# Thirteen Strassen pairs instead of eight in the up product of an FFN, and the gate product moved behind a spill

## The chip, the core and the metric

The kernel runs on one core of a Trainium2 chip. Its engines work side by side, each with a queue that it takes in order: TensorE (PE: matmul, with its weight loads as PEld), VectorE (DVE), ScalarE (ACT), GpSimd (POOL), and SyncE (SP), which issues the DMAs. A scheduler fixes the order in each queue when the program is built. The metric is the device time of one launch in microseconds; the kernel before takes 855.47 us, the median of three runs from 853.64 to 856.37.

## The reference, cut to what matters

One layer over 512 tokens of width 1024: a mixer (an mLSTM branch and an S5 branch), a residual with layer norm, and then a feed-forward block with a causal convolution of three taps on its gate:

```python
FFN_HIDDEN = ((8 * D_MODEL // 3 + 127) // 128) * 128      # 2816 = 22 tiles of 128
def _conv_glu_ffn(h, w_ffn_up, w_ffn_conv, b_ffn_conv, w_ffn_down):
    val, gate = jnp.split(h @ w_ffn_up, 2, axis=-1)
    gate = jax.nn.gelu(_causal_dwconv(gate, w_ffn_conv, b_ffn_conv))
    return (gate * val) @ w_ffn_down
...
    x = _layer_norm(ALPHA * x + (1.0 + g1) * mix, ln1_gain[l], ln1_bias[l])
    h = _standardize(x) * (1.0 + sc2) + sh2
    f = _conv_glu_ffn(h, w_ffn_up[l], w_ffn_conv[l], b_ffn_conv[l], w_ffn_down[l])
    x = _layer_norm(ALPHA * x + (1.0 + g2) * f, ln2_gain[l], ln2_bias[l])
```

sh1 to g2 are six rows of 1024 that come from a second input c by a matrix (w_ada); g2 is one of them and multiplies the block's result.

## The kernel before

**Arithmetic.** Every large product is taken in three passes: each fp32 operand is split into a rounded high part (an ACT cast, L226 for weights) and a low part (a DVE subtraction, L215), and mm3 (L247 to L249) adds high·high, high·low and low·high. Weights come by DMA into a tile w, which wsplit turns into wh and wl.

**Stages.** The mixer takes the first 440 us. Then tail_product runs the mix product, a running sum over k whose last steps are kept back so that the four token tiles t = 0 to 3 end one after the other; finish1 adds the residual x (two loads of 256 KB into hx for each tile) and norms it (post), and h2tr transposes the result, the first half of the tokens and then the second half. The up product follows. Its 22 hidden tiles are called pairs here: pair j has a gate tile and a value tile of 128 rows each. Pairs 0 and 1 are computed in token halves while the norm of the last tile still runs; 2 and 3 are ordinary pairs, which is 48 matmuls of 512 columns. From j = 4 on, fast_and_plain takes a Strassen pair and an ordinary one together, eight times, with their matmuls interleaved. A Strassen pair is seven products (prod, L1287) of 12 matmuls of 256 columns, 84 in all; its weights are combined by four DVE operations (fast_operands) and each of the seven operands is split by half (an ACT cast, L1250, and a DVE subtraction). The gate goes through gate_half (bias, convolution with two DVE operations, gelu2 with two more and two on ACT) and is multiplied by the value in val_half, on DVE. The results of pairs 0 to 17 are spilled to DRAM; 18 to 21 stay on the chip as split operands.

**Down product.** tail_product again, over the 22 pairs in the order 18, 19, 0 to 17, 20, 21: 14 steps of 24 matmuls, and eight that are kept back. act_at loads a spilled pair and splits it; scaled multiplies each row of down weights by g2 with two DVE operations before the split. finish2 and post add the residual and norm.

**g2.** Its row is summed on DVE from 16 loads (ada2_step, part q = 3: a tensor_scalar L201 at kc = 0, then scalar_tensor_tensor L207), spread over the up product by MODS, and grow_in_place (four matmuls, L963, with casts and splits on both sides) spreads the sum over the partitions at j = 16.

**What sets the order.** Tile pools: a load waits until the tile that last had its slot has been read (hh has 7 slots, s5h 8, w 2, hb 6). PSUM banks are acc (2), s5 (2) and hd (4). SP takes its DMAs in order, so one that waits for a slot holds up all that are behind it.

Of the kernel before, what the change touches and what calls it, by code (L numbers as in the profile page):

```python
# [162 lines left out]
def _build(ctx, tc, nc, h):  # L163
# [1054 lines left out]

    def gate_half(j, og):
# [12 lines left out]
        gelu2(gg, a, lambda: bank("hd"))  # L1232
        return gg

    def val_half(j, gg, ov):
# [6 lines left out]
        if j < NSP:  # L1242
            dma(spill[j * P:(j + 1) * P, :], gg)
            gp_.append(None)
        else:
            gp_.append(pair_of(gg, "hb" if j < 20 else "gab"))
# [53 lines left out]
    def fast_and_plain(j):  # L1300
        src = fast_operands(j)
        b, d = gtile[j % 2], vtile[j % 2]
        g2_, v2_ = gtile[1 - j % 2], vtile[1 - j % 2]
        a, c = bank("hd"), bank("hd")
        cv = hh()

        def part(o, w, n):
            for k in range(4 * n, 4 * n + 4):
                sl = slice(k * P, (k + 1) * P)
                mm3(o, w[0][:, sl], w[1][:, sl], h2[k][0], h2[k][1], k == 0, k == KD - 1)  # L1310

        prod(a, half(src[0]), xq(0, 0), True)
        A.copy(b[:, 0:256], a[:, 0:256])
        prod(c, half(src[1]), xc(3), True)
        A.copy(cv[:, 0:256], c[:, 0:256])
        wg_ = wsplit(h["wup"][2 * j + 3])
        part(g2_, wg_, 0)
        prod(b, half(src[2]), xc(2))
        tt(d[:, 0:256], b[:, 0:256], cv[:, 0:256], ALU.add)
        prod(a, half(src[3]), xq(1, 0))  # L1320
        part(g2_, wg_, 1)
        prod(b, half(src[4]), xc(1))
        tt(cv[:, 256:512], b[:, 0:256], cv[:, 0:256], ALU.add)
        prod(d, half(src[5]), xc(4))
        gg2 = gate_half(j + 1, (g2_,))
        wv_ = wsplit(h["wup"][2 * j + 2])
        part(v2_, wv_, 0)
        prod(b, half(src[6]), xq(1, 1))
        gg = gate_half(j, (a, b))
        val_half(j, gg, (d, cv[:, 256:512]))  # L1330
        part(v2_, wv_, 1)
        val_half(j + 1, gg2, (v2_,))
# [81 lines left out]
```

## Time and profile before

| | |
|---|---|
| median of three runs | 855.47 us |
| the profiled execution | 858.85 us |
| its span, first to last instruction | 857.1 us |
| mean granted TensorE clock | 0.995 of full speed |
| PE, DVE, ACT busy | 820.4, 656.0, 386.6 us |
| up product, pairs 4 to 19 | 532.9 to 704 us |
| down product | 726.8 to 849.5 us |

A share of busy time is a mean over stages with different limits. A matmul's row gives its whole way through the array, so matmuls overlap in the records; what one costs in a full stream is the distance from its start to the start of the next. The same holds for DVE: in a full queue its instructions start a little closer than they are long.

### The profile page before, as it was taken

How to read it: one execution, taken by the hardware profiler on the slowest of the kernel's cores; microseconds unless marked ns; L12 is line 12 of the kernel's file. 1: busy time of each engine (PE TensorE's matmuls, PEld its weight loads, DVE VectorE, ACT ScalarE, POOL GpSimd, SP SyncE). 2: the span in 40 equal slices, each digit the busy share in tenths (PEclk: the TensorE clock that was granted, in tenths of full speed). 3: DMA queues.
4: the chain of work that ended last, by engine and by line, in shares of the span. 5: the costliest groups of instructions: out<-in, count | busy, mean ns of one | idle time of the engine just before them, and what ended most of it. 6: DMA issues, size and time to landing. Idle time of an engine off the chain costs nothing.

```text
span 857.1 us, 12135 instructions
## 1 busy us (share of the span) xinstructions
PE 820.4 (96%) x4394; PEld 676.6 (79%) x4394; DVE 656.0 (77%) x1273; ACT 386.6 (45%) x647; POOL 96.4 (11%) x233
## 2 busy tenths in 40 slices
PE   3999999999999999999999999999999999999996
PEld 1777868778777778888887987899988888888885
DVE  5557978778689775568988899989888766999044
ACT  4454573564557442332334475455554544555000
POOL 2781221122022100000001200000000000000000
PEclk9999999999999999999999999999999999999998
DMA  9832132122212333558656016445443322677011
GB/s 340 286 133 87 52 103 62 44 88 62 80 56 82 97 124 121 181 188 300 212 180 206 13 50 240 165 148 174 151 167 103 114 68 98 228 236 247 2 50 49
DMA packets 50604, 115.44 MB, mean 135 GB/s; under 512 B 13936, under 2 KB 14832, under 8 KB 50544
## 3 DMA queue, kind: packets, MB, share of 16 engines
q1 hardware_dynamic: 50544, 114.67, 39.6%
q8 instruction: 34, 0.56, 0.3%
q14 instruction: 26, 0.21, 0.1%
HBM read 105.73 MB, written 6.82 MB: 131 GB/s over the span
## 4 chain that ended last, share of the span: by engine, by line
PE 69%; DVE 16%; DMA 5%; ACT 4%; issue 3%; SPq 2%; POOL 1%; DVEq 0%; ACTq 0%; POOLq 0%
PE acc L247 9%; PE acc L248 9%; PE acc L249 9%; PE hd L247 7%; PE hd L249 7%; PE hd L248 7%; DVE hh L207 4%; PE s L247 3%; PE s L249 3%; PE hd L1287 3%; PE s L248 3%; PE acc L1287 3%; DMA hh<-in_wa 3%; DVE wl L215 2%; SPq L197 2%
## 5 line engine op out<-in xcount | busy, mean ns | idle before, releaser
L226 ACT CAST wh<-w 128x1024 fp32r<-128x1024 f32 (+2 forms) x87 | 86.6, 998 | 116.0 <-PE acc L248 75.0
L215 DVE TENSOR_TENSOR wl<-w,wh 128x1024 fp32r<-128x1024 f32 (+2 forms) x87 | 101.0, 1163 | 24.9 <-ACT wh L226 24.1
L247 PE MATMUL acc<-hp,wh 128*128 128x512 f32 x256 | 103.4, 405 | 0.4 <-ACT hx L790 0.4
L249 PE MATMUL acc<-hp,wl 128*128 128x512 f32 x256 | 102.1, 399 | 0.0
L248 PE MATMUL acc<-hp,wh 128*128 128x512 f32 x256 | 102.0, 399 | 0.0
L1041 POOL TENSOR_SCALAR mov<-mov 128x1 f32<-128x1 f32 x6 | 3.7, 609 | 500.6 <-ACT acc L1040 327.6
L247 PEld LDWEIGHTS acc<-hp,wh 128*128 128x128 f32 x256 | 48.2, 189 | 14.7 <-issue 3.7
L249 PEld LDWEIGHTS acc<-hp,wl 128*128 128x128 f32 x256 | 48.3, 189 | 11.2 <-issue 0.4
L248 PEld LDWEIGHTS acc<-hp,wh 128*128 128x128 f32 x256 | 48.4, 189 | 10.8 <-issue 0.4
L207 DVE SCALAR_TENSOR_TENSOR s5h<-hh,k,s5h 128x512 f32<-128x512 f32 x56 | 39.7, 747 | 8.8 <-DMA hh<-in_wa 8.8
L207 DVE SCALAR_TENSOR_TENSOR hh<-hd,hh 128x512 f32<-128x512 f32 (+3 forms) x38 | 22.9, 603 | 15.8 <-POOL hh L859 8.4
L247 PE MATMUL hd<-s5b,wh 128*128 128x512 f32 (+1 forms) x88 | 31.8, 367 | 0.7 <-ACT s5b L1203 0.5
L248 PE MATMUL hd<-s5b,wh 128*128 128x512 f32 (+1 forms) x88 | 32.1, 366 | 0.2 <-DVE s5b L215 0.2
L249 PE MATMUL hd<-s5b,wl 128*128 128x512 f32 (+1 forms) x88 | 32.1, 366 | 0.0
L1250 ACT CAST hb<-hx 128x512 fp32r<-128x512 f32 x32 | 19.9, 622 | 25.4 <-PE acc L1287 14.4
L248 PE MATMUL acc<-hx,wh 128*128 128x512 f32 x76 | 30.0, 395 | 0.0
L247 PE MATMUL acc<-hx,wh 128*128 128x512 f32 x76 | 29.9, 394 | 0.0
L249 PE MATMUL acc<-hx,wl 128*128 128x512 f32 x76 | 29.9, 393 | 0.0
L226 ACT CAST hb<-hh 128x512 fp32r<-128x512 f32 (+3 forms) x39 | 21.5, 553 | 16.4 <-DVE hh L207 11.1
L212 DVE TENSOR_TENSOR hh<-w,s5h 128x512 f32<-128x512 f32 x42 | 27.4, 685 | 0.0
L215 DVE TENSOR_TENSOR hb<-hh,hb 128x512 fp32r<-128x512 f32 (+3 forms) x39 | 23.3, 604 | 3.9 <-ACT hb L226 3.6
L1287 PEld LDWEIGHTS acc<-hp,hb 128*128 128x128 f32 x192 | 24.9, 188 | 1.6 <-DVE s L212 0.5
(600 smaller groups left out, 2286.6 us busy)
## 6 DMA issues: line engine op xcount, KB each, us to landing
hh<-in_wa SPq DMA_DIRECT2D x64, 256.0 KB, 4.5
w<-in_win SPq DMA_DIRECT2D x30, 512.0 KB, 3.2
w<-in_wup SPq DMA_DIRECT2D x28, 512.0 KB, 3.5
w<-in_wfd SPq DMA_DIRECT2D x22, 512.0 KB, 3.3
hb<-in_wa SPq DMA_DIRECT2D x16, 512.0 KB, 6.9
gab<-in_wup SPq DMA_DIRECT2D x16, 512.0 KB, 3.7
spill<-hh SPq DMA_DIRECT2D x18, 256.0 KB, 2.4
hh<-spill SPq DMA_DIRECT2D x18, 256.0 KB, 3.7
```

The lines of the kernel that those rows point to most:

```text
L197: return nc.sync.dma_start(o, i)
L207: V.scalar_tensor_tensor(o, i0, s, i1, op0=op0, op1=op1)
L212: V.tensor_tensor(o, a, b, op=op)
L215: V.tensor_tensor(o, a, b, op=ALU.subtract)
L226: A.copy(hi, x)
L247: T.matmul(o, lhsT=wh, rhs=xh, start=first, stop=False)
L248: T.matmul(o, lhsT=wh, rhs=xl, start=False, stop=False)
L249: T.matmul(o, lhsT=wl, rhs=xh, start=False, stop=last)
L1041: GP.tensor_scalar(v[:, 2:3], v[:, 0:1], v[:, 1:2], EPS * D, op0=ALU.add, op1=ALU.add)
L1250: A.copy(o[:, 0], src)
L1287: T.matmul(o[:, 0:256], lhsT=w[:, p, sl], rhs=x[k][y], start=first and k + i == 0, stop=k == 3 and i == 2, skip_group_check=True)
```

## The change

The Strassen pairs are now 4, 5, 6, 8, 9, 10, 12, 13, 14, 16, 17, 18 and 20; ordinary are 0 to 3, 7, 11, 15, 19 and 21. group(j0, m) takes m Strassen pairs and, if j0 is not in PURE, the ordinary pair after them; the ordinary pair sums in an hd bank instead of acc and s5. Pairs 0 to 18 spill gate and value separately (the value is copied out of PSUM by ACT), and act_at loads both and multiplies. The down weights are no longer scaled by g2; post multiplies the sum by it. Only pair 19 is still on the chip when the down product starts. grow_in_place moves from j = 16 to j = 21, and the 16 loads of q = 3 go into s5h slots and stand in the list of steps from the start.

```diff
-G2J = 16
-FAST = (4, 6, 8, 10, 12, 14, 16, 18)
+FAST = {4: 2, 6: 1, 8: 2, 10: 1, 12: 2, 14: 1, 16: 2, 18: 1, 20: 1}
+PURE = (4, 8, 12, 16)
 XJ = 3
-MODS = (4, 6, 6, 8, 10, 10, 12, 14)
-NSP = 18
+MODS = (8, 12, 14, 16, 18, 18, 20, 20)
+NSP = 19
...
-    steps = [(q, kc) for q in (2, 0, 1) for kc in range(KD)]
+    steps = [(q, kc) for q in (2, 0, 1, 3) for kc in range(KD)]
...
-                acc2[q] = [s5h(), s5h()]
+                acc2[q] = [XB4[:, i * 512:(i + 1) * 512] for i in range(2)] if q == 3 else [s5h(), s5h()]
             for i, a in enumerate(acc2[q]):
-                wi = hh()
+                wi = s5h() if q == 3 else hh()
...
     def scaled(src, g, st, tags=("wh", "wl")):
+        if g is None:
+            return wsplit(src, tags=tags)
...
             for i, (n, c_) in enumerate(cut):
-                stt(r[n][:, c_], res[n][:, c_], ALPHA, bk[n][:, c_])
-                if tail is not None and i == len(cut) - 1:
-                    tt(r[n][:, c_], r[n][:, c_], tail[:, 0:c_.stop - c_.start], ALU.add)
+                y = bk[n]
+                far = tail is not None and i == len(cut) - 1
+                if scale is not None:
+                    tt(r[n][:, c_], y[:, c_], scale[n][:, c_])
+                    y = r[n]
+                stt(r[n][:, c_], res[n][:, c_], ALPHA, y[:, c_])
+                if far:
+                    e_ = hh(c_.stop - c_.start)
+                    tt(e_, tail[:, 0:c_.stop - c_.start], scale[n][:, c_])
+                    tt(r[n][:, c_], r[n][:, c_], e_, ALU.add)
                 add(i)
...
-        gelu2(gg, a, lambda: bank("hd"))
+        gelu2(gg, a, lambda: gg)
...
-    def val_half(j, gg, ov):
+    def val_half(j, gg, ov, room=None):
+        if j < NSP:
+            if len(ov) == 1:
+                v = hh()
+                A.copy(v, ov[0])
+            else:
+                v = room
+                A.copy(v[:, 0:256], ov[0][:, 0:256])
+            dma(spill[j * P:(j + 1) * P, :], gg)
+            dma(spillv[j * P:(j + 1) * P, :], v)
+            gp_.append(None)
+            return
...
-    def fast_and_plain(j):
...
+    def group(j0, m):
+        js = range(j0, j0 + m)
+        jn = j0 + m
+        src = [fast_operands(j) for j in js]
...
+        def quarter(i):
+            e, n = divmod(i, 2)
+            if n == 0:
+                nw[e] = wsplit(h["wup"][2 * jn + 1 - e])
+                no[e] = bank("hd")
...
+        def fourth(i, j):
+            prod(b[j], half(src[i][6]), xq(1, 1))
+            gg = gate_half(j, (a[j], b[j]))
+            val_half(j, gg, (d[j], cv[j][:, 256:512]), cv[j])
+
+        gn = None
+        for q, part in enumerate((first, second, third)):
+            for i, j in enumerate(js):
+                part(i, j)
+                if i == 0 and j0 not in PURE:
+                    quarter(q)
+                    if q == 1:
+                        gn = gate_half(jn, (no[0],))
+        for i, j in enumerate(js):
+            fourth(i, j)
+            if i == 0 and j0 not in PURE:
+                quarter(3)
+                val_half(jn, gn, (no[1],))
...
-    steps.extend((3, kc) for kc in range(KD))
     first = []
     for j in range(NF):
-        if j == G2J:
+        if j == FJ:
             g2 = grow_in_place(1, 0.5, "hd")
         if j >= FJ:
-            first.append(scaled(h["wfd"][18 + len(first)], g2, None))
+            first.append(scaled(h["wfd"][19 if not first else 0], None, None))
...
-    down = [18, 19] + list(range(NSP)) + [20, 21]
+    down = [19] + list(range(NSP)) + [20, 21]
...
             dma(x, spill[j * P:(j + 1) * P, :])
-            got[kk] = pair_of(x, "hx" if j % 6 < 3 else "s5h")
+            v = hh()
+            dma(v, spillv[j * P:(j + 1) * P, :])
+            tt(x, x, v)
+            got[kk] = pair_of(x, "hx" if j % 7 < 3 else "s5h")
...
-    tail_product(act_at, [h["wfd"][j] for j in down], g2, "hh", NF, 8, [("s5b", "s5b")] * 2 + [("hp", "hp")] * 4 + [("hb", "hb")] * 2, finish2, FDB, first, far=True)
+    tail_product(act_at, [h["wfd"][j] for j in down], None, "hh", NF, 8, [("s5b", "s5b")] * 2 + [("hp", "hp")] * 4 + [("hb", "hb")] * 2, finish2, FDB, first, far=True)
```

**SP queue, end of the mix product.** The two loads of x for the last token tile are hx_1036 and hx_1037. In the kernel before they stand right behind those of tile 2 (hx_993, hx_994):

```order
L197 DMA hx_993_4690<-in_x 128x512 [waits DMAHW7_49]
L197 DMA hx_994_4691<-in_x 128x512
L197 DMA hx_1036_4843<-in_x 128x512 [waits DVE_49]
L197 DMA hx_1037_4844<-in_x 128x512 [waits DMAHW7_49,DMAHW2_49,DVE_49]
L197 DMA w_1111_5315<-in_wup 128x1024 [waits DMAHW5_49,DMAHW3_49,DVE_49]
```

In the change (in_wa2 is the matrix of g2):

```order
L197 DMA hx_993_4690<-in_x 128x512 [waits DMAHW7_49]
L197 DMA hx_994_4691<-in_x 128x512
L197 DMA s5h_1226_6162<-in_wa2 128x512 [waits PE_49]
L197 DMA hx_1036_4843<-in_x 128x512 [waits DMAHW2_49,DVE_49]
L197 DMA hx_1037_4844<-in_x 128x512 [waits DMAHW7_49,DMAHW3_49,DVE_49]
L197 DMA s5h_1227_6165<-in_wa2 128x512 [waits PE_49]
L197 DMA s5h_1296_6660<-in_wa2 128x512 [waits DMAHW5_49,DMAHW1_49,DVE_49]
L197 DMA s5h_1297_6663<-in_wa2 128x512 [waits DMAHW6_49,DMAHW4_49,DVE_49]
```

A load of q = 3 has come between, into an s5h slot that a matmul of the mix product must have left (the wait on PE), and a second one behind.

**DVE queue, norm of the last token tile.** hx_1039 to hx_1042 are its residual sum and its normed halves, k_37_148 is the sum of q = 3. Before:

```order
L215 TENSOR_TENSOR hx_1019_4732<-hh_1035_4785,hx_1018_4731 128x256 [waits Activation_49]
L207 SCALAR_TENSOR_TENSOR hx_1039_4848<-hx_1036_4843,acc_926_4384 128x512 [waits DMAHW1_49]
L1056 BN_STATS qst_1043_4852<-hx_1039_4848 128x6 [waits DVE_49]
L207 SCALAR_TENSOR_TENSOR hx_1040_4849<-hx_1037_4844,acc_927_4385 128x256 [waits DMAHW2_49,PE_49]
L207 SCALAR_TENSOR_TENSOR hx_1040_4849<-hx_1037_4844,acc_927_4385 128x256
L1056 BN_STATS qst_1043_4852<-hx_1040_4849 128x6 [waits DVE_49] x2
L1059 BN_AGGR qmv_1044_4853<-qst_1043_4852 128x2 [waits DVE_49]
L201 TENSOR_SCALAR mom_1045_4854<-qmv_1044_4853 128x1 [waits DVE_49]
```

In the change:

```order
L215 TENSOR_TENSOR hx_1019_4732<-hh_1035_4785,hx_1018_4731 128x256 [waits Activation_49]
L201 TENSOR_SCALAR k_37_148<-s5h_1226_6162,k_15_92 128x512 [waits DMAHW1_49]
L207 SCALAR_TENSOR_TENSOR hx_1039_4848<-hx_1036_4843,acc_926_4384 128x512 [waits DMAHW2_49]
L1059 BN_STATS qst_1043_4852<-hx_1039_4848 128x6 [waits DVE_49]
L207 SCALAR_TENSOR_TENSOR hx_1040_4849<-hx_1037_4844,acc_927_4385 128x256 [waits DMAHW3_49,PE_49]
L207 SCALAR_TENSOR_TENSOR hx_1040_4849<-hx_1037_4844,acc_927_4385 128x256
L1059 BN_STATS qst_1043_4852<-hx_1040_4849 128x6 [waits DVE_49] x2
L201 TENSOR_SCALAR k_37_148<-s5h_1227_6165,k_15_92 128x512 [waits DMAHW4_49]
L1062 BN_AGGR qmv_1044_4853<-qst_1043_4852 128x2 [waits DVE_49]
L207 SCALAR_TENSOR_TENSOR k_37_148<-s5h_1296_6660,k_15_92,k_37_148 128x512 [waits DMAHW5_49]
L201 TENSOR_SCALAR mom_1045_4854<-qmv_1044_4853 128x1 [waits DVE_49]
```

Three steps of q = 3 stand in the chain shown, each behind its own load; two more (s5h_1297_6663 and s5h_1328_6880) stand further down on both sides of the second BN_AGGR, ahead of hx_1054, which the transposes read.

**PE queue, the two ends of the up product.** hb_1399 is pair 19's product as a split operand, wh_1448 the down weights of pair 19, hb_1413 the first operand of Strassen pair 20, hx_1460 the first spilled pair after its load, k_50 the ones by which grow_in_place spreads g2. Before, the last value tile (s5_1059) is followed by 48 matmuls of the two pairs on the chip:

```order
L248 MATMUL s5_1059_4898<-hx_1019_4732,wh_1400_7285 128x512
L249 MATMUL s5_1059_4898<-hx_1018_4731,wl_1401_7286 128x512
L247 MATMUL acc_1403_7317<-wh_1391_7235,hb_1378_7140 128x512
L248 MATMUL acc_1403_7317<-wl_1392_7236,hb_1378_7140 128x512
L249 MATMUL acc_1403_7317<-wh_1391_7235,hb_1378_7140 128x512
L247 MATMUL acc_1404_7318<-wh_1391_7235,hb_1378_7140 128x512 [waits DVE_49,Activation_49]
```

In the change, at the end of pair 19's value tile (hd_1394):

```order
L249 MATMUL hd_1394_7325<-hx_1018_4731,wl_1393_7322 128x512
L247 MATMUL acc_1450_7652<-wh_1448_7648,hb_1399_7381 128x512 [waits Activation_49]
L248 MATMUL acc_1450_7652<-wl_1449_7649,hb_1399_7381 128x512 [waits DVE_49]
L247 MATMUL s5_1452_7654<-wh_1448_7648,hb_1399_7381 128x512
L1309 MATMUL hd_1410_7408<-s5b_1008_4721,hb_1413_7411 128x256 [waits Activation_49]
```

and at the end of the up product:

```order
L249 MATMUL hd_1428_7551<-hx_1018_4731,wl_1427_7548 128x512
L249 MATMUL acc_1450_7652<-wh_1448_7648,hb_1399_7381 128x512
L247 MATMUL acc_1451_7653<-wh_1448_7648,hb_1399_7381 128x512 [waits Activation_49]
L248 MATMUL acc_1451_7653<-wl_1449_7649,hb_1399_7381 128x512
L249 MATMUL acc_1451_7653<-wh_1448_7648,hb_1399_7381 128x512
L249 MATMUL s5_1452_7654<-wh_1448_7648,hb_1399_7381 128x512
L964 MATMUL hd_1440_7626<-hh_1441_7627,k_50_183 128x512 [waits Activation_49]
L964 MATMUL hd_1440_7626<-hh_1442_7628,k_50_183 128x512 [waits DVE_49]
L964 MATMUL hd_1444_7637<-hh_1445_7638,k_50_183 128x512 [waits Activation_49]
```

In the change PE's first down step (pair 19) begins in front of pair 20, and the rest of its 24 matmuls, with the four of grow_in_place, are all that stands between the up product and the first spilled pair.

**DVE queue, in the change, the last rows ahead of that pair** (hh_1422 and hh_1432 are the products of 21 and 20, hx_1461 its low part):

```order
L207 SCALAR_TENSOR_TENSOR k_37_148<-hd_1440_7626,hh_1439_7624 128x512 [waits DMAHW3_49,PE_49]
L212 TENSOR_TENSOR hh_1432_7586<-s5_1058_4898,hh_1432_7586 128x256 [waits DVE_49]
L212 TENSOR_TENSOR hh_1432_7586<-hh_1412_7410,hh_1432_7586 128x256
L201 TENSOR_SCALAR k_37_148<-k_37_148 128x512 [waits DVE_49]
L215 TENSOR_TENSOR hh_1446_7639<-k_37_148,hh_1445_7638 128x512 [waits Activation_49]
L215 TENSOR_TENSOR gab_1433_7593<-hh_1432_7586,gab_1433_7593 128x512 [waits Activation_49]
L215 TENSOR_TENSOR gab_1434_7609<-hh_1422_7509,gab_1434_7609 128x512 [waits Activation_49]
L207 SCALAR_TENSOR_TENSOR k_37_148<-hd_1444_7637,hh_1443_7635 128x512 [waits DMAHW5_49,PE_49]
L201 TENSOR_SCALAR k_37_148<-k_37_148 128x512 [waits DVE_49]
L212 TENSOR_TENSOR hh_1458_7660<-hh_1458_7660,hh_1459_7662 128x512 [waits DMAHW7_49,DMAHW6_49,DMAHW1_49]
L215 TENSOR_TENSOR wl_1482_7783<-w_1480_7780,wh_1481_7782 128x1024 [waits DMAHW2_49,Activation_49]
L215 TENSOR_TENSOR hx_1461_7666<-hh_1458_7660,hx_1460_7665 128x512 [waits Activation_49]
```

Ahead of the first row shown stand pair 21's product, a split of down weights (wl_1475), the first split of grow_in_place (hh_1442) and the two last steps of pair 20's gelu. Pair 20's product, the rest of grow_in_place, three splits, the first multiplication of a spilled pair (hh_1458) and another split of down weights (wl_1482) follow, all ahead of hx_1461.

## Rows read from the trace of the kernel before

**Rows 1.** The page: busy time by engine, and the chain that ended last.

```profile
PE 820.4 (96%) x4394; PEld 676.6 (79%) x4394; DVE 656.0 (77%) x1273; ACT 386.6 (45%) x647; POOL 96.4 (11%) x233
...
PE 69%; DVE 16%; DMA 5%; ACT 4%; issue 3%; SPq 2%; POOL 1%; DVEq 0%; ACTq 0%; POOLq 0%
```

**Rows 2.** Stretches, each: length; busy time of PE, PEld, DVE, ACT, POOL; clock; DMA share; GB/s.

```profile
532.00:704.00 172.00, 170.16 (x1058) 152.22 (x1059) 142.68 (x225) 86.42 (x148) 0.00 (x0) 1.00 0.42 141
...
727.00:850.00 123.00, 122.55 (x552) 100.09 (x551) 81.95 (x140) 38.22 (x69) 2.95 (x6) 1.00 0.40 137
```

**Rows 3.** PE's waits from 440 us on: waiting line, releaser, total us, times, longest.

```profile
PE acc L247 <- DVE hh L207: 1.9, 1, 1.9
PE hd L963 <- DVE hh L215: 0.9, 1, 0.9
```

**Rows 4.** Timeline of PE in the up product: start us, length us, line, operation, tiles, count.

```profile
566.81 1.60 PE L1287 MATMUL s<-hp,hb 128*128 128x256 f32 x12
568.25 0.40 PE L247 MATMUL s<-s5b,wh 128*128 128x512 f32 x1
...
571.03 1.22 PE L1287 MATMUL acc<-s5h,hb 128*128 128x256 f32 x9
...
572.44 0.40 PE L247 MATMUL s<-s5h,wh 128*128 128x512 f32 x1
```

**Rows 5.** DVE by line and shape, 507 to 704 us: count, busy us, mean ns, idle before.

```profile
L215 DVE TENSOR_TENSOR wl<-w,wh 128x1024 fp32r<-128x1024 f32 x22 | 26.8, 1218 | 6.0 <-ACT wh L226 6.0
L215 DVE TENSOR_TENSOR hb<-hx,hb 128x512 fp32r<-128x512 f32 x32 | 21.8, 684 | 0.3 <-ACT hb L1250 0.3
...
L207 DVE SCALAR_TENSOR_TENSOR hh<-acc,k,hh 128x511 f32<-128x511 f32 x10 | 7.4, 744 | 0.0
```

**Rows 6.** Timeline of DVE at the start of the down product, a full queue.

```profile
726.49 0.68 DVE L212 TENSOR_TENSOR hh<-w,s5h 128x512 f32<-128x512 f32 x1
727.09 0.68 DVE L212 TENSOR_TENSOR hh<-s,hh 128x512 f32<-128x512 f32 x1
```

**Rows 7.** ACT by line and shape, 507 to 727 us.

```profile
L226 ACT CAST wh<-w 128x1024 fp32r<-128x1024 f32 x24 | 25.0, 1047 | 26.4 <-PE acc L248 17.3 <-DMA w<-in_wup 4.6 <-PE s L248 4.3
L1250 ACT CAST hb<-hx 128x512 fp32r<-128x512 f32 x32 | 19.9, 622 | 25.4 <-PE acc L1287 14.4 <-PE hd L1287 5.0 <-PE s L1287 4.9
...
L567 ACT ACTIVATE hd<-hh 128x512 f32<-128x512 f32 x22 | 13.2, 599 | 17.1 <-DVE hh L207 17.1
```

**Rows 8.** DMA issues from 467 to 475 us: count, KB, median us to landing.

```profile
hx<-in_x SPq DMA_DIRECT2D x2, 256.0 KB, 3.4
```

**Rows 9.** Timeline of SP: issue of the last x loads; the last of them.

```profile
471.29 0.33 SPq L197 DMA_DIRECT2D hx<-in_x  x1
```

**Rows 10.** Timeline of DVE, norm of the last token tile.

```profile
482.98 0.68 DVE L207 SCALAR_TENSOR_TENSOR hx<-hx,acc 128x512 f32<-128x512 f32 x1
...
491.33 1.00 DVE L203 TENSOR_SCALAR hx<-hx,mom,rs 128x512 f32<-128x512 f32 x2 [0.76 <-POOL rs L1061]
```

**Rows 11.** Timeline of PE: last step of the mix product; the transposes of the second half.

```profile
480.80 0.28 PE L249 MATMUL acc<-gab,s5h 128*128 128x256 f32 x1
...
492.27 0.60 PE L1192 MATMUL s<-k,hx 128*128 128x128 f32 x4
```

**Rows 12.** Timeline of PE: the first matmul of the down product.

```profile
726.82 0.40 PE L247 MATMUL acc<-wh,hb 128*128 128x512 f32 x1
```

**Rows 13.** Stretches, columns as in rows 2: after a wait at 161.5, and after one at 470.

```profile
160.70:164.10 3.40, 2.60 (x17) 2.59 (x17) 3.35 (x7) 2.03 (x4) 0.00 (x0) 0.80 0.02 5
164.10:170.00 5.90, 5.90 (x31) 5.35 (x31) 2.47 (x3) 1.10 (x2) 0.00 (x0) 0.83 0.36 98
470.00:476.00 6.00, 5.66 (x31) 4.80 (x32) 4.68 (x14) 3.59 (x9) 2.05 (x4) 1.00 0.27 97
```

**Rows 14.** Timeline of PE: the wait ahead of that stretch.

```profile
161.50 0.46 PE L617 MATMUL s<-k,s5b 128*128 128x128 f32 x2 [1.65 <-DVE k L215]
```

**Rows 15.** Timeline of DVE after the last matmul.

```profile
849.59 0.42 DVE L212 TENSOR_TENSOR hh<-hh,acc 128x256 f32<-128x256 f32 x1 [1.75 <-PE acc L249]
```

More of the change, by code (lines that the diff above doesn't have):

```diff
@@ L573, in _build @@
     XB = const([P, 2, 4, 2, K5])
+    XB4 = XB.rearrange("p a b c d -> p (a b c d)")
     GP.memset(XB, 0.0)
@@ L1065, in quick, with post @@
         return add, close
-    def post(t, bk, gain, bias, res, alloc, sums=None, tail=None):
+    def post(t, bk, gain, bias, res, alloc, sums=None, scale=None, tail=None):
         r, o = ([alloc(), alloc()] for _ in range(2))
@@ L1071, in post @@
             for n in range(2):
-                stt(r[n], res[n], ALPHA, bk[n], acc=s_[:, n:n + 1])
+                y = bk[n]
+                if scale is not None:
+                    tt(r[n], y, scale[n])
+                    y = r[n]
+                stt(r[n], res[n], ALPHA, y, acc=s_[:, n:n + 1])
             nm = mean_of(s_)
@@ L1078, in post @@
             for i, (n, c_) in enumerate(cut):
[L1079 to L1081 removed]
+                y = bk[n]
+                far = tail is not None and i == len(cut) - 1
+                if scale is not None:
+                    tt(r[n][:, c_], y[:, c_], scale[n][:, c_])
+                    y = r[n]
+                stt(r[n][:, c_], res[n][:, c_], ALPHA, y[:, c_])
[3 more added lines that the diff above has]
+                    tt(r[n][:, c_], r[n][:, c_], e_, ALU.add)
                 add(i)
@@ L1215, in _build @@
     spill = dp.tile([NSP * P, 512], F32, name="spill")
+    spillv = dp.tile([NSP * P, 512], F32, name="spillv")
     gtile = [bank("acc"), bank("acc")]
@@ L1241, in val_half @@
                 tt(gg[:, sl], ov[i][:, 0:256], gg[:, sl])
[L1242 to L1246, printed above, removed]
+        gp_.append(pair_of(gg, "hb" if j < 20 else "gab"))
     def half(src):
@@ L1298, in fast_operands @@
         return a11, r3, r2, a12, r1, a22, r4
-    def fast_and_plain(j):
[L1301 to L1307, printed above, removed]
+    def group(j0, m):
+        js = range(j0, j0 + m)
+        jn = j0 + m
+        src = [fast_operands(j) for j in js]
+        a, c, b, d, cv = {}, {}, {}, {}, {}
+        nw, no = {}, {}
+        def quarter(i):
[3 more added lines that the diff above has]
+                no[e] = bank("hd")
@@ L1308, in part @@
             for k in range(4 * n, 4 * n + 4):
                 sl = slice(k * P, (k + 1) * P)
[L1310 to L1332, printed above, removed]
+                mm3(no[e], nw[e][0][:, sl], nw[e][1][:, sl], h2[k][0], h2[k][1], k == 0, k == KD - 1)
@@ new lines, in first, with second @@
+        def first(i, j):
+            a[j], c[j] = bank("hd"), bank("hd")
+            b[j], d[j] = gtile[j % 2], vtile[j % 2]
+            cv[j] = hh()
+            prod(a[j], half(src[i][0]), xq(0, 0), True)
+            A.copy(b[j][:, 0:256], a[j][:, 0:256])
+            prod(c[j], half(src[i][1]), xc(3), True)
+            A.copy(cv[j][:, 0:256], c[j][:, 0:256])
+        def second(i, j):
+            prod(b[j], half(src[i][2]), xc(2))
+            tt(d[j][:, 0:256], b[j][:, 0:256], cv[j][:, 0:256], ALU.add)
+            prod(a[j], half(src[i][3]), xq(1, 0))
@@ new lines, in third @@
+        def third(i, j):
+            prod(b[j], half(src[i][4]), xc(1))
+            tt(cv[j][:, 256:512], b[j][:, 0:256], cv[j][:, 0:256], ALU.add)
+            prod(d[j], half(src[i][5]), xc(4))
+        def fourth(i, j):
[10 more added lines that the diff above has]
+                        gn = gate_half(jn, (no[0],))
@@ L1354, in _build @@
         if j in FAST:
-            fast_and_plain(j)
-        elif j - 1 not in FAST:
+            group(j, FAST[j])
+        elif not any(f < j < f + m + (f not in PURE) for f, m in FAST.items()):
             ou = {}
@@ L1375, in finish2 @@
                 ts(l2[0][n], l2[0][n], math.sqrt(D))
-        r = yield from post(t, bk, l2[0], l2[1], x1[t], hh, tail=tail)
+        r = yield from post(t, bk, l2[0], l2[1], x1[t], hh, scale=g2, tail=tail)
         for n in range(2):
```

## The prediction

> **What bounds the kernel now.** I read the page first: PE is busy for 820.4 of 857.1 us, and 69% of the chain that ended last is PE [rows 1]. Then the stretches: in the pairs 4 to 19 PE is busy for 170.16 of 172 us and DVE for 142.68; in the down product PE for 122.55 of 123 us and DVE for 81.95 [rows 2]. So work taken off PE comes out of the time if PE gets its operands in time, and DVE has slack in the mean only. PE's waits from 440 us on are few: 1.9 us behind a gate tile whose bank the last convolution of pair 3 still reads, and 0.9 us in grow_in_place, are the two that the change touches [rows 3]. Whoever reads such a kernel should ask where PE's next operand comes from whenever a stage ends, since there the other engines have no lead.
>
> I take the distances of starts: 0.23 us for a matmul of 512 columns (12 of them from 568.25 to 571.03, 2.78 us), 1.425 us for 12 of 256 (1.44 from 566.81, 1.41 from 571.03) [rows 4]. On DVE a 128x512 operation is 0.68 long and costs 0.60 in a full queue [rows 6]; by the same 0.08 off the others cost 1.14 (weight row, 1218 ns), 0.66 (scalar_tensor_tensor, 744 ns) [rows 5], 0.34 (256 columns, 0.42) [rows 15] and 0.46 (tensor_scalar, two in 1.00) [rows 10].
>
> **The change part by part.**
>
> *Five more Strassen pairs.* An ordinary pair is 4 x 2.78 = 11.12 us of PE, a Strassen pair 7 x 1.425 = 9.98. Five of them give 5 x 1.14 = 5.7 us. The rows show both widths costing the same per column.
>
> [...]
>
> *DVE in the groups.* A Strassen pair costs DVE four combinations and seven low parts (11 x 0.60), two sums (0.68), and two convolution and two gelu steps (4 x 0.66): 9.9 us beside PE's 9.98, now without the product with the value (ACT copies it). The ordinary pair costs 2 x 1.14 + 4 x 0.66 = 4.9 of 11.1. A pure group of two has no slack, the mixed ones have 6. In three Strassen pairs and one ordinary pair, which is the new pattern, DVE has 34.6 of 41.1 us, so it falls behind only inside a pure group; by the same sums along both queues operands are ready some 5 us ahead there. I take 0; the bounds are 0 and 4 us (1 for each of four pure groups). The second spill of each pair, 256 KB in about 13 us more, lies on queues that are 42% busy [rows 2], and gelu's scratch, now in place, only frees PSUM: both 0.
>
> *Waits that go.* The ordinary pair now sums in an hd bank, so the 1.9 us go: its matmul no longer follows the convolution of pair 3. The first operand of pair 4 is next, and DVE reaches it well before. The 0.9 us go with grow_in_place. Together 2.8; if something else comes late there, 0.9.
>
> *End of the mix product.* Before, the loads of x for the last token tile were issued by 471.29 and landed about 3.4 us later [rows 8, 9], eight before DVE read them at 482.98 [rows 10]. Now a load of g2's matrix stands ahead of them on SP, and its slot is free only after the last step of the mix product, whose matmuls run to about 481.0 [rows 11]. Its issue and theirs follow then, 0.45 apart; 3.4 us later is 484.9, so the residual starts 1.9 us late. Behind it DVE takes four more steps in the chain (0.46 + 3 x 0.66 = 2.4), of which the 0.76 idle ahead of the norm hides about 0.6. The norm, which stood at 491.33, starts 3.7 us late. PE reaches the transposes at 492.27 without a gap [rows 11], 0.4 after their operand: it loses 3.3. What is queued behind the waiting rows on DVE is that norm itself, on SP the weights of pair 2, which wait for their slots anyway. Bounds 2.0 (loads land in 2.5 us, the steps hide) and 4.5.
>
> *Start of group 20.* PE's first down matmuls stand behind pair 19's last one and in front of pair 20. ACT must first take a weight cast (1.05, its slot is left by that same matmul), a Square (0.60) and the cast of pair 19's product (0.62) [rows 7]: 2.1 to 2.3 us in which PE, in order, waits. Bounds 1.3 (without the weight cast) and 2.6.
>
> *Start of the down product.* Before, the first down matmul follows without a gap [rows 12], and 48 of them, 11.1 us, pass before a spilled pair is needed. Now 20 of pair 19 and four of grow_in_place are left, 24 x 0.2325 = 5.6 us. From the last matmul of the up product DVE must take, in order: pair 21's product 0.60, weights 1.14, gelu steps and ends of grow_in_place 4 x 0.66 + 2 x 0.46, sums of pair 20 0.68, four splits 2.4, the spilled pair's product 0.60: 9.0 us, and ACT's cast 0.62. PE starts on it at 9.6, 4.0 late. Each handover between engines adds a little: 5.1; if the scheduled steps of grow_in_place overlap better, 3.0.
>
> *Down product otherwise.* DVE loses two scalings for each k and gains one product, 0.60 less; both lie beside PE. DMA moves 1 MB for each k of 5.6 us instead of 0.77: about 188 GB/s for 137 [rows 2]. I take 0, at most 1. act_at asks for spilled pairs three steps, 17 us, ahead.
>
> *Tail.* After the last matmul one more operation of 256 columns: 0.4 [rows 15]. For the other tiles the multiplications lie beside matmuls.
>
> Sum: -5.7 - 2.8 + 3.3 + 2.1 + 4.0 + 0.4 = +1.3 us on the profiled execution, whose 858.85 us stands 3.4 above the median of 855.47. From the median: 856.8 us. With every unknown at its good end (2.0, 1.3, 3.0) -2.1, at its bad end (4.5, 2.6, 5.1, groups 4, DMA 1, 0.9 of the waits only) about +11.
>
> **The rivals.**
>
> *The stages' ends cost little.* My walks assume that DVE stands idle until its row is due. If the scheduler's order leaves ACT and DVE earlier than I sum, as at 726.82, where DVE was in a full queue and PE saw no gap [rows 6, 12], only group 20 and the tail cost: -8.5 + 2.5 = -6.0, 849.5 us; with half of the other two, -2.3 and 853.1. Against it: before, PE had twice the cover there. It decides where fewer than 6 us of DVE work are left at the last up matmul.
>
> *DVE becomes the bound in the pure groups.* 9.9 beside 9.98 leaves nothing for handovers; once the 5 us of prepared operands are used, PE runs at DVE's pace. 1 us for each of four groups puts the time at 860.8. It decides from the second half of a pure group on. For it: with one Strassen pair in two, DVE is at 142.68 of 172 us already [rows 2]. Against it: each pure group follows one with slack.
>
> [...]
>
> [...]
>
> [...]
>
> **How the numbers follow.** About 0.3% (2.6 us) is what a measurement can tell here from no change, so faster is below 852.9 and slower above 858.0. Forecast (no change that can be told, 853.4 to 860 by its own bounds): 0.46. Stage ends cheap: 0.28. DVE bound in the pure groups: 0.14. Half clock: 0.11. Spacing: 0.01. Faster takes most of the second, 0.27; slower the last three and 0.13 of the forecast's upper end, 0.38; the same 0.35. The range, 849 to 863, leaves out the far ends of the outer cases.
>
> **What would show it.** Right: PE's waits list a wait near 3 us on the transposes of the second half, with x loads landing after the last mix matmul; about 2 us on the first down matmul behind pair 19; about 4 us in the first 10 us of the down product, released by DVE and ACT; none at the first matmul of pair 4; 13 x 84 matmuls at 0.119 apart. Wrong: waits spread over the pure groups, or a granted clock below 1 after the waits, or transposes that start as early as before.

## The result, and the profile after

The change takes 863.09 us, the median of four executions from 861.48 to 865.06; the kernel before, run beside it, takes 855.12. The ratio is 1.0095, with a 95% interval from 1.0076 to 1.0114: eight microseconds slower. I had forecast 856.8, no change that can be told, with a range up to 863.0 and a chance of 0.38 for slower. The time lies 0.1 us outside.

The page of the change, busy time and the chain that ended last, answers to [rows 1]:

```profile
PE 817.4 (95%) x4574; PEld 682.5 (79%) x4574; DVE 657.9 (77%) x1265; ACT 406.5 (47%) x689; POOL 96.8 (11%) x233
...
PE 60%; DVE 22%; ACT 6%; DMA 6%; issue 4%; SPq 1%; POOL 1%; DVEq 0%; ACTq 0%; POOLq 0%
```

PE is busy 3 us less than before, and yet the span is 2.7 longer: what the pairs gave is lost in waits. PE's share of the chain is 9 points smaller, and 8 of them are now DVE's and ACT's. PE's five longest waits from 440 us on answer to [rows 3], in the same columns:

```profile
PE s L1206 <- DVE hx L203: 2.6, 1, 2.6
PE acc L247 <- ACT hb L226: 1.9, 1, 1.9
PE acc L247 <- ACT hx L226: 1.7, 1, 1.7
PE hd L964 <- ACT hh L226: 1.5, 2, 0.8
PE hd L964 <- DVE hh L215: 0.9, 1, 0.9
```

The first is the norm of the last token tile, the second the first down matmul behind pair 19, and the last three the start of the down product: 2.6, 1.9 and 4.1 us. The 1.9 us in front of pair 4 are gone, and so is the 0.9 where grow_in_place stood.

**The profile that I read was itself one that took longer than most.** A second profiled execution of the kernel before (b_again) took 854.24 us, where the first had taken 858.85; if a profiled execution of this kernel were always longer, it should have come to 858 to 859 again. Here is the last step of the mix product in b_again and then in the change; before it stood at 480.80 [rows 11]. All of that stretch is code that the change doesn't touch.

```profile
477.05 0.28 PE L249 MATMUL acc<-gab,s5h 128*128 128x256 f32 x1
```

```profile
478.33 0.28 PE L249 MATMUL acc<-gab,s5h 128*128 128x256 f32 x1
```

So 3.75 of the 4.6 us between the two executions of one kernel lie in the first stage. In the thirteen profiles that this text reads that stage took from 477.2 to 480.9 us, and the first profile has the longest of them. By stages, from the starts of PE's matmuls, with the end of the last one as the end of the down product (us; e5, e12 and e11 are versions told below; some 1.7 us of an execution's time lie outside its profiled span):

| stage | before, first | before, second | change | e5 | e12 | e11 |
|---|---|---|---|---|---|---|
| start to the first matmul of pairs 0 and 1 | 480.9 | 477.2 | 478.5 | 479.0 | 477.8 | 479.7 |
| to the first matmul of pair 2 | 27.0 | 27.0 | 30.6 | 30.7 | 31.2 | 27.0 |
| to the end of the up product | 219.0 | 218.1 | 212.5 | 215.5 | 210.9 | 211.7 |
| down product | 122.7 | 122.7 | 130.5 | 122.9 | 122.6 | 122.6 |
| after the last matmul | 7.6 | 7.5 | 7.7 | 7.6 | 7.7 | 7.6 |
| time of this execution | 858.85 | 854.24 | 861.48 | 857.55 | 851.78 | 850.45 |

Against the second execution the stages that the change touches cost +3.62 - 5.57 + 7.81 + 0.11 = +6.0; the first stage adds 1.3.

**The norm of the last token tile.** SP and DVE of the change, answering to [rows 9] and [rows 10]:

```profile
478.53 0.33 SPq L197 DMA_DIRECT2D s5h<-in_wa  x1
478.95 0.85 SPq L197 DMA_DIRECT2D hx<-in_x  x2
```

```profile
481.46 0.49 DVE L201 TENSOR_SCALAR k<-s5h,k 128x512 f32<-128x512 f32 x1 [0.87 <-DMA s5h<-in_wa]
482.19 0.69 DVE L207 SCALAR_TENSOR_TENSOR hx<-hx,acc 128x512 f32<-128x512 f32 x1 [0.25 <-DMA hx<-in_x]
...
492.21 1.00 DVE L203 TENSOR_SCALAR hx<-hx,mom,rs 128x512 f32<-128x512 f32 x2 [0.65 <-POOL rs L1064]
```

The loads leave SP as soon as the mix product's last step lets go of the slot, DVE stands 0.87 us for the first of them, and the last norm starts 13.9 us after that step, where it took 10.5 before.

**The granted clock** (stretches, columns as in [rows 2]; the clock is the third number from the end):

```profile
490.00:495.00 5.00, 1.83 (x9) 1.41 (x8) 3.78 (x11) 1.42 (x3) 1.12 (x2) 0.82 0.32 105
495.00:500.00 5.00, 5.00 (x38) 4.84 (x37) 4.15 (x11) 4.15 (x9) 0.00 (x0) 0.84 0.02 3
725.00:730.00 5.00, 4.20 (x9) 2.99 (x10) 4.16 (x9) 1.86 (x4) 0.00 (x0) 0.53 0.85 258
730.00:735.00 5.00, 3.35 (x11) 2.33 (x9) 2.37 (x4) 1.56 (x2) 0.00 (x0) 0.79 0.72 222
```

From 493.5 to 496.5 us the clock reads 0.50 throughout, and 1.00 from 497 on; that is the half level. A mean of 0.82 in 5 us is 1.8 us at it; together the first two rows hold 3.4 us of it and the last two 6.8. Neither stretch was below 1.00 before.

**The start of the down product** (PE, DVE and ACT of the change, answering to [rows 12]; 721.33 is the last matmul of the up product, and the down product goes on at 721.56):

```profile
721.33 0.40 PE L249 MATMUL hd<-hx,wl 128*128 128x512 f32 x1
...
723.67 0.51 PE L964 MATMUL hd<-hh,k 128*128 128x512 f32 x1 [0.79 <-ACT hh L226]
...
725.10 0.63 PE L964 MATMUL hd<-hh,k 128*128 128x512 f32 x1 [0.92 <-DVE hh L215]
...
726.43 0.79 PE L964 MATMUL hd<-hh,k 128*128 128x512 f32 x1 [0.71 <-ACT hh L226]
...
727.02 0.63 PE L247 MATMUL hd<-wh,hb 128*128 128x512 f32 x1
...
731.10 0.69 DVE L207 SCALAR_TENSOR_TENSOR k<-hd,hh 128x512 f32<-128x512 f32 x1 [1.85 <-PE hd L964]
...
732.14 0.41 PE L249 MATMUL hd<-wh,hb 128*128 128x512 f32 x1
732.17 0.69 DVE L212 TENSOR_TENSOR hh<-hh,hh 128x512 f32<-128x512 f32 x1
...
733.28 1.04 ACT L226 CAST wh<-w 128x1024 fp32r<-128x1024 f32 x1 [5.00 <-PE hd L249]
734.23 0.61 ACT L226 CAST hx<-hh 128x512 fp32r<-128x512 f32 x1
...
734.90 0.50 PE L247 MATMUL acc<-wh,hx 128*128 128x512 f32 x1 [1.66 <-ACT hx L226]
```

Three waits for grow_in_place; then twelve matmuls that take 5.12 us, from 727.02 to 732.14, where twelve took 2.78 in [rows 4]; then a wait for the cast of the first spilled pair. That pair's product was ready at 732.86, but ACT had a cast of weights ahead of it, and that one waited for its slot until PE had ended the first step; the pair's own cast began at 734.23, so 1.4 of the last 1.66 us stand on ACT's queue. From 721.56 to 734.90 PE did what takes 5.6 us in a full stream: 7.8 lost.

The tail, answering to [rows 15], has one operation more, as expected, 0.46 apart:

```profile
852.14 0.42 DVE L212 TENSOR_TENSOR hh<-acc,k 128x256 f32<-128x256 f32 x1 [1.07 <-PE acc L249]
852.60 0.42 DVE L212 TENSOR_TENSOR hh<-hh,hh 128x256 f32<-128x256 f32 x1
```

### The profile page after: what moved, and what is told of

Read it like the earlier page. It is cut to its first block, busy times and chain, and to the rows that moved or that the text cites. A ratio compares the mean times of both kernels' runs of the same rounds, so it can differ in the third digit from the quotient of the medians.

```text
span 859.8 us, 12663 instructions
## 1 busy us (share of the span) xinstructions
PE 817.4 (95%) x4574; PEld 682.5 (79%) x4574; DVE 657.9 (77%) x1265; ACT 406.5 (47%) x689; POOL 96.8 (11%) x233
## 4 chain that ended last, share of the span: by engine, by line
PE 60%; DVE 22%; ACT 6%; DMA 6%; issue 4%; SPq 1%; POOL 1%; DVEq 0%; ACTq 0%; POOLq 0%
PE acc L247 8%; PE acc L248 7%; PE acc L249 7%; PE hd L247 7%; PE hd L248 7%; PE hd L249 7%; DVE hh L207 5%; DVE hb L215 3%; PE hd L1309 2%; DVE hx L212 2%; PE acc L1309 2%; PE s L247 2%; PE s L248 2%; PE s L249 2%; DMA gab<-in_wup 2%
## 5 line engine op out<-in xcount | busy, mean ns | idle before, releaser
L247 PE MATMUL hd<-s5b,wh 128*128 128x512 f32 (+1 forms) x128 | 48.1, 380 | 0.7 <-ACT s5b L1217 0.5
L248 PE MATMUL hd<-s5b,wh 128*128 128x512 f32 (+1 forms) x128 | 48.3, 377 | 0.2 <-DVE s5b L215 0.2
L249 PE MATMUL hd<-s5b,wl 128*128 128x512 f32 (+1 forms) x128 | 48.2, 377 | 0.0
L1309 PE MATMUL acc<-hp,hb 128*128 128x256 f32 x312 | 41.8, 282 | 0.3 <-DVE s L212 0.3
L207 DVE SCALAR_TENSOR_TENSOR hh<-hh,hh 128x512 f32<-128x512 f32 x52 | 35.8, 689 | 7.9 <-ACT hh L567 3.1
L1309 PEld LDWEIGHTS acc<-hp,hb 128*128 128x128 f32 x312 | 39.6, 188 | 1.8 <-DVE s L212 1.0
L1272 ACT CAST hb<-hx 128x512 fp32r<-128x512 f32 x52 | 32.0, 621 | 14.1 <-PE acc L1309 7.0
L215 DVE TENSOR_TENSOR hb<-hx,hb 128x512 fp32r<-128x512 f32 x52 | 35.4, 687 | 1.3 <-ACT hb L1272 0.8
L215 DVE TENSOR_TENSOR hb<-gab,hb 128x512 fp32r<-128x512 f32 x39 | 26.8, 687 | 2.6 <-ACT hb L1272 2.4
L247 PEld LDWEIGHTS hd<-s5b,wh 128*128 128x128 f32 x128 | 24.1, 191 | 5.5 <-ACT s5b L1217 0.8
L248 PEld LDWEIGHTS hd<-s5b,wh 128*128 128x128 f32 x128 | 24.5, 192 | 4.7 <-DVE s5b L215 0.6
L249 PEld LDWEIGHTS hd<-s5b,wl 128*128 128x128 f32 x128 | 24.4, 190 | 4.6
```

The source lines that it names most:

```text
L207: V.scalar_tensor_tensor(o, i0, s, i1, op0=op0, op1=op1)
L215: V.tensor_tensor(o, a, b, op=ALU.subtract)
L247: T.matmul(o, lhsT=wh, rhs=xh, start=first, stop=False)
L248: T.matmul(o, lhsT=wh, rhs=xl, start=False, stop=False)
L249: T.matmul(o, lhsT=wl, rhs=xh, start=False, stop=last)
L1272: A.copy(o[:, 0], src)
```

## The experiments

Theory A: the pairs give what the rows say, and the waits at the stages' ends, with the half clock behind them, take it and more. Rivals: the loss is in the exchange itself (DVE the bound in the pure groups), or in the value product that moved into the down product. Where a kernel ran in several executions its ratio to the kernel before on the same chip is given with its interval.

**The loads of g2's matrix back in hh slots** (e1_hh; e1_again is the same kernel once more):

```diff
-                wi = s5h() if q == 3 else hh()
+                wi = hh()
```

> The change, but the loads of g2's matrix go into hh slots again, so that none stands ahead of the last x loads. Theory A (the new waits cost their length and a stretch at half clock each): the wait of 2.6 us at the transposes goes and the granted clock stays 1.00 between 485 and 505 us; 863.1 - 3.6 = 859.5 us. Theory B (the waits cost their length only, and the clock falls whatever stands there): 860.5 us, and a stretch under 1.00 remains within 485 to 505 us.

> The loads of g2's matrix in hh slots, once more, for its profile: its time fell by 1 us only where the walk gives 2.6 and theory A 3.6. Theory A: the transposes come 2.6 us earlier and the clock is full there, but another stretch at half clock stands elsewhere (start of the down product). Rival: the loads, now on hh slots, hold up something else, and a wait of 1 to 2 us stands in the up product that the change has not.

1.0078 (1.0059 to 1.0097), a little over 1 us less than the change: a miss for theory A, and nearer to B's time. The profile of e1_again (859.40 us) shows why, and it doesn't speak for B. The transposes wait 0.3 us instead of 2.6, and the clock is 1.00 from 485 to 505 us, as theory A said. But the loads, now held up by hh slots, come late: the last is issued at 719.69 us, in the change at 592.94. DVE, with the steps of q = 3 still to do, makes PE wait at the start of the down product in place of the transposes (PE's longest wait), and the half clock stands there (third number from the end):

```profile
PE s L247 <- DVE hh L212: 4.0, 1, 4.0
```

```profile
720.00:725.00 5.00, 2.44 (x4) 1.12 (x4) 4.94 (x9) 2.21 (x4) 0.00 (x0) 0.52 0.67 227
725.00:730.00 5.00, 4.98 (x12) 3.93 (x13) 3.52 (x6) 0.07 (x1) 0.00 (x0) 0.50 0.81 261
```

**Two pairs on the chip** (e2_two: NSP = 18, and the down product begins with 18 and 19):

```diff
-NSP = 19
+NSP = 18
...
-            first.append(scaled(h["wfd"][19 if not first else 0], None, None))
+            first.append(scaled(h["wfd"][18 + len(first)], None, None))
...
-    down = [19] + list(range(NSP)) + [20, 21]
+    down = [18, 19] + list(range(NSP)) + [20, 21]
```

> The change, but with pair 18 kept on the chip too: two direct pairs at the start of the down product (48 matmuls of cover). Theory A: the waits at the start of the down product go (k = 1 no longer 1.7 us late, those of grow_in_place remain in part) and with them the stretches at half clock; from the last up matmul to the last matmul 7.8 us less than in the change at best, 863.1 - 6 = 857 us. Theory B (half clock comes whatever the waits are): only 1.7 us, 861.4. Rival (DVE is behind by more than the cover): unchanged, 863.

1.0086 (1.0071 to 1.0101). The first spilled pair was no longer waited for, as theory A says, but the time went to the down step in front of pair 20:

```profile
PE acc L247 <- ACT hb L226: 5.6, 1, 5.6
```

**grow_in_place at pair 19, its sums earlier** (e3_grow):

```diff
-MODS = (8, 12, 14, 16, 18, 18, 20, 20)
+MODS = (6, 8, 10, 12, 14, 14, 16, 16)
...
-        if j == FJ:
+        if j == 19:
             g2 = grow_in_place(1, 0.5, "hd")
```

> The change, but grow_in_place runs at pair 19 instead of 21 and its sums are due two to four pairs earlier: DVE has 3.4 us less ahead of the first spilled pair, and PE no waits inside its first down step. Theory A: the four waits at the start of the down product (4.1 us) shrink to about 0.6, the clock stays 1.00 there, and about 0.9 us of waiting appears where grow_in_place now stands: 863.1 - 6 = 857 us. Theory B: 863.1 - 3.5 + 0.9 = 860.5, half clock stays.

1.0054 (1.0034 to 1.0074), 859.36 us: 3.7 us less than the change, between theory A's 6 and theory B's 2.6. At the start of the down product two waits of 1.1 us were left, with 0.73 of the clock from 730 to 735 us.

**Matmuls in the wait at the transposes** (e4_fill):

```diff
         if hv:
+            idle = bank("s5")
+            for i in range(12):
+                T.matmul(idle[:, 0:256], lhsT=early[0][1][0][:, 0:P], rhs=h2[0][0][:, 0:256], start=True, stop=True)
             h2tr(1)
```

> The change with 12 more matmuls of 256 columns (1.4 us at full clock) in front of the transposes of the second token half, into a bank that nothing reads: the wait there is as long as before, but PE works in half of it. Theory A (the idle time in the wait takes the clock down): clock 1.00 from 485 to 505 us and 1 to 1.7 us less than the change, 861.7. Theory B (the clock falls for another reason there, such as the small transposes): same stretch under 1.00, 863.1 or a little more.

862.41 us, 1.0091 (1.0062 to 1.0119): too near the change to tell by the time alone. The profile tells: 1.2 us of the wait is left, and the same stretches as in the change above read

```profile
490.00:495.00 5.00, 3.19 (x23) 2.35 (x21) 3.78 (x10) 1.79 (x4) 1.13 (x2) 1.00 0.34 108
495.00:500.00 5.00, 5.00 (x40) 4.69 (x41) 4.93 (x14) 3.92 (x9) 0.00 (x0) 1.00 0.00 0
```

In the change, with a wait of 2.6 us there, these stretches have 0.82 and 0.84, and in e12, with 2.8 us, 0.98 and 0.68; here PE was at work in half of it, and both have 1.00. One execution, but with theory A, and e1_again, where the wait was 0.3 us, kept 1.00 there too. The other three executions of e4 took 861.40 to 864.99 us with a mean clock of 0.989 to 0.995; where they lost it isn't recorded. From the first matmul of pairs 0 and 1 to pair 2 the profiled one took 30.0 us, the change 30.6: by these two executions the stretch at half clock costs about 0.6 us there and not 1.7, the half of its 3.4. That PE waits for DVE and ACT in part of it would explain that; it wasn't tried.

**Matmuls in the first down step** (e13_fill2: ten of 512 columns, ahead of its first matmul):

```diff
+            if far and k == 0:
+                for i in range(10):
+                    T.matmul(bk[3][1], lhsT=h2[0][0][:, 0:P], rhs=h2[0][0], start=True, stop=True)
```

> The change with ten more matmuls of 512 columns (2.3 us at full clock) in the first step of the down product, into a bank before it is used; most stand in the midst of grow_in_place. If the first spilled pair waits for ACT's queue (a weight cast that needs the slot of the first step's own weights stands ahead of its cast), the wait at the second step stays 1.7 us though the first step ends later. If it waits for DVE's queue, as the walk had it, the wait shrinks to 0. If idle time takes the clock down, the stretch below 1.00 from 725 to 735 us goes or halves: 861.7 us or less; if not, 865.

864.89 us, one execution. It didn't isolate what I wanted: the added matmuls stand behind the waits of grow_in_place, the clock had fallen by then (0.80 and 0.51 in the same two stretches), and in this kernel the two casts on ACT stand the other way round:

```profile
735.28 0.62 ACT L226 CAST hx<-hh 128x512 fp32r<-128x512 f32 x1 [4.50 <-DVE hh L212]
...
738.17 1.05 ACT L226 CAST wh<-w 128x1024 fp32r<-128x1024 f32 x1 [2.27 <-PE hd L249]
```

With the pair's cast ahead of the weights', PE had no wait at the second step. That fits ACT's queue as the cause, which the rows of the change show directly; by itself this run doesn't settle it, since the added work also gave DVE more time.

**Eight pairs again** (e5_old):

```diff
-FAST = {4: 2, 6: 1, 8: 2, 10: 1, 12: 2, 14: 1, 16: 2, 18: 1, 20: 1}
+FAST = {4: 1, 6: 1, 8: 1, 10: 1, 12: 1, 14: 1, 16: 1, 18: 1}
-PURE = (4, 8, 12, 16)
+PURE = ()
```

> The change with the eight Strassen pairs of the kernel before (4, 6, ... 18), each with an ordinary pair; all else as in the change. Five pairs more cost PE 11.12 instead of 9.98: +5.7; the down step in front of pair 20 goes: -1.9. If the exchange is worth what the rows say: 863.1 + 3.8 = 866.9 us. Rival (DVE is the bound in the pure groups, so that the exchange is worth nothing): 861 to 863.

1.0012 (0.9999 to 1.0024): 6 to 7 us *less* than the change, a plain miss. It looked as if five pairs more cost time. But its profile has no wait over 0.3 us behind the first matmuls of pair 2, the start of the down product included, and its only long one is that of the transposes:

```profile
PE s L1206 <- DVE hx L203: 2.5, 1, 2.5
```

With pair 20 ordinary, grow_in_place and the weights for pair 19 are put between pairs 20 and 21 instead of behind both. I had undone two things at once: the number of pairs, and the group that ends the up product. It also clears the value product and the scaling: all of that is in this kernel too, and its down product takes 122.9 us, where the kernel before takes 122.7.

**Only pair 20 ordinary again** (e12_no20):

```diff
-FAST = {4: 2, 6: 1, 8: 2, 10: 1, 12: 2, 14: 1, 16: 2, 18: 1, 20: 1}
+FAST = {4: 2, 6: 1, 8: 2, 10: 1, 12: 2, 14: 1, 16: 2, 18: 1}
```

> The change with pair 20 ordinary again, twelve Strassen pairs, nothing else. The waits in front of pair 20 (1.9 us) and at the start of the down product (4.1 us, and 3.7 by half clock) go, the exchange of one pair is lost (+1.1), the wait of 2.6 us at the transposes stays: 863.1 - 8.6 = 854.5 us. Rival (the loss is in the pure groups or in the down product as a whole): 861 to 864.

852.35 us, 0.9964 (0.9947 to 0.9980): faster than before, with four pure groups and twelve pairs. The waits at both ends of pair 20 are gone and the clock is full where the change had 0.53:

```profile
725.00:730.00 5.00, 5.00 (x23) 4.07 (x22) 4.07 (x6) 2.41 (x4) 0.00 (x0) 1.00 0.94 334
```

This is the run that decides: the last Strassen pair, with the order of work that comes with it, costs about 11 us (1.0095 against 0.9964). And beside e5 it prices the exchange: the two kernels differ only in their Strassen pairs, eight or twelve, and both end with pairs 20 and 21 ordinary. The up product takes 215.5 us with eight and 210.9 with twelve, 4.6 less, and the rows gave 4 x 1.14 = 4.6; the whole times differ by about 4.1 us (1.0012 against 0.9964).

**Three edits with the down product begun by a spilled pair** (e10_pre: hh slots, grow_in_place at 19, spilled pair 0 loaded ahead of group 20; MODS is that of e3, and first stays empty, so that no down weights are split ahead of the down product):

```diff
-    down = [19] + list(range(NSP)) + [20, 21]
+    down = list(range(NSP)) + [19, 20, 21]
...
+        if j == 20:
+            act_at(0, 1)
```

> The change with three edits: loads of g2's matrix in hh slots, grow_in_place at pair 19, and the down product begins with spilled pair 0, which is loaded and multiplied ahead of group 20; pair 19 is taken with 20 and 21 at its end. If the waits at the stages' ends and the stretches at half clock behind them are what the change lost: the down product follows within 1 us, no stretch under 1.00 from 480 to 850 us, 854 to 856 us. Rival (the loss is in the exchange itself or in the rest of the down product): 859 or more.

863.67 us, 1.0072 (1.0045 to 1.0099): a miss. Its first down matmuls stand in front of pair 20 again, and with grow_in_place there as well; the clock is 0.50 from 705 to 710 us. The profiled execution is the longest of the five, 866.57 us:

```profile
PE acc L247 <- ACT hx L226: 4.4, 2, 3.4
PE hd L964 <- ACT hh L226: 2.5, 1, 2.5
PE hd L964 <- DVE hh L215: 1.7, 2, 1.0
```

**Twelve pairs and the two early edits** (e11_twelve: as e12, with hh slots, grow_in_place at 19 and MODS = (4, 6, 8, 10, 10, 12, 14, 16)):

> Twelve Strassen pairs (pair 20 ordinary again), the loads of g2's matrix in hh slots and due from pair 4 on, grow_in_place at pair 19; the rest as in the change. If the change loses at its stages' ends what it gains in the pairs: 4 x 1.14 = 4.6 us for four pairs more and 1.9 for the wait in front of pair 4, no new wait over 1 us and no stretch at half clock between 480 and 840 us: 855 - 6.5 = 848.5 us. Rival (exchanged pairs are worth nothing by themselves, or the value product by the spill costs time in the down product): 853 to 856.

849.42 us, 0.9930 (0.9912 to 0.9949), the best of all and near the 848.5 expected: 0.7% less than the kernel before. No wait over 0.85 us is left from 440 us on, the first of the list being one that the kernel before has too, and the clock is 1.00 up to the last matmul:

```profile
PE acc L247 <- ACT wh L226: 0.8, 1, 0.8
```

**Thirteen pairs, the last group ahead of pair 20** (e15_last: as e11, with 18: 2). In this kernel the products of pairs 19 and 20 meet each other's down weights: the same work, on the wrong weights.

> As the version with twelve pairs, but thirteen: the last group is pairs 18 and 19 with the ordinary pair 20, and 21 is ordinary. One exchange more is worth 1.1 us; PE has pair 21 as cover behind the last group, so that the start of the down product keeps its lead; the first down matmuls stand in front of pair 21's tiles and may wait up to 2 us: 847.5 to 849.5 us. Rival (the waits of the change come back with the late Strassen pair): 853 or more.

853.34 us, 0.9980 (0.9965 to 0.9995), 4 us more than e11. The rival: a late group of two brings waits back, here 1.1 and 1.0 us and smaller ones, and 0.71 of the clock from 725 to 730 us.

```profile
PE acc L247 <- ACT hx L226: 1.1, 1, 1.1
PE hd L1309 <- ACT hh L1345: 1.0, 1, 1.0
```

## Why the prediction was wrong

The step that failed is the start of the down product: 4.0 us in the sum, 7.8 measured, because PE stood where my walk had it run, and because the sum put the half clock behind the waits at nothing. The touched stages cost +6.0 us against the second execution before, where I had +1.3. Of these 4.7 us too little, 3.8 are in that term and 0.8 in the up product. By the medians the change costs 8.0 us. The last 2.0 aren't located in anything the change touches: 1.3 lie in the first stage of these two executions, and the rest between each of them and its median.

**The exchange: right.** e12 and e5 give 4.6 us for four pairs, as the rows had it. The 0.01 for spacing stands for an exchange that gains nothing on PE; no run shows such a spacing: [rows 4] have 0.23 us at 512 columns and 0.119 at 256. DVE as the bound of the pure groups did not appear either: the longest wait between pair 4 and pair 19 is 0.3 us in the change, which has four of these groups.

**Norm of the last tile: right.** 3.3 forecast; 2.6 of waiting and 3.6 for the stage, 0.6 of it by the clock if e4 is taken as the measure.

**Start of group 20: right.** 2.1 forecast, 1.95 measured.

**Start of the down product: mis-sized**, 4.0 forecast and 7.8 measured. The waits are 4.1, but not those of my walk. I let PE run through its 24 matmuls while DVE worked down its queue. In fact PE stood for grow_in_place three times, DVE then stood 1.85 us for the fourth of its matmuls, which had been queued behind eight others, and the spilled pair's cast stood behind ACT's cast of weights. And the clock fell, to 0.53 from 725 to 730 us: a stretch as in [rows 13] comes to 1.7 us, and here the half clock cost 2.3 on the twelve matmuls alone, and more by the DVE step that waits for one of them. e4, the same code there but with 3.4 us at half clock instead of 6.8, needed 12.2 us where the change needed 13.3.

**Half clock: it came true along with the forecast.** I made it a case of its own with 0.11, as if it excluded the walk. Here it came with the walk's own waits: behind the one at the transposes, 2.6 us, the change has 0.82 and 0.84, and with the 4.1 us at the start of the down product 0.53 and 0.79. I held it unlikely because full streams run around these waits; but from 490 to 495 us PE was busy for only 1.83 of 5.00, a smaller share than the 2.60 of 3.40 at 161 [rows 13], where the clock was 0.80 behind a wait of 1.65 us [rows 14]. e12 agrees at the transposes: 0.98 and 0.68 behind 2.8 us. In e2, e3, e5 and e13 the wait there is 3.0, 2.9, 2.5 and 2.9 us; their mean clocks over the whole span are 0.990, 0.990, 0.993 and 0.989, where b_again, without such a wait, has 0.998.

**From the profiled execution to the median: this step held.** I took 3.4 us off because the profiled execution stood that far above the median, without knowing where they lay. b_again shows it: 3.75 us more in the first stage, which the change leaves alone. Without that step my forecast would have been 860.2, nearer to the 863.09, but by luck. Against the first execution the change's first stage was 2.5 us shorter and its touched stages cost 5.1, where I had +1.3. The other three executions of the change had a mean clock of 0.987 where the profiled one had 0.991, and took 1.5 to 3.6 us more; where their half clock lay isn't recorded, so that part is left open.

**Which part of the change loses.** I had taken the late Strassen pair and the two ends as separate terms. e12 shows them as one: pair 20 gains 1.1 us and brings 1.95 and 7.8 with it. A group is emitted whole, so everything that was meant to run between pairs 20 and 21 came behind both. That this order, and not the Strassen product itself, is what costs is argued and not shown: e3, which moved grow_in_place and its sums alone, got 3.7 us back, but no run kept pair 20 a Strassen pair with all of that work in between.

Two of the prediction's sums are off, without weight for the forecast: the good end of its terms is -1.8 us and not -2.1, and the chances that it adds up for slower make 0.39 and not 0.38.

## What to carry to other kernels

Look at what a stage's last piece of work leaves for the engines behind PE: a faster product at the end of a stage can cost more than all before it gain (here about 11 us, against 4.6 for four pairs), and undoing just that piece is the first experiment to make. When a forecast holds a new wait of PE like those at the transposes here (2.6 us in the change, 2.8 in e12, with 0.82 and 0.84, 0.98 and 0.68 of the clock behind them), price a stretch at half clock with it, and not as a rival to it. Compare stage by stage against more than one execution of the kernel before, and check first that the untouched stages agree.

## What the runs showed of the hardware

The waits in front of pair 20 in the change and before pair 4 in the kernel before, both 1.9 us, left the clock at 1.00 (700 to 710 us in the change, 533 to 540 before), as did those in e4 and e1_again, while in front of the same pair 1.9 us in e3 and in e13 were followed by 0.66 from 700 to 705 us, and 5.6 us in e2 by 0.50 from 705 to 710. So in the change and in e13, whose added matmuls come later, a wait of the same length went either way. That four executions of the change spread over 3.6 us may come from it; it wasn't tried.
